# Dilated attention in a decoder trunk: Q and K of six head pairs made in a seven-product phase ahead of the heads, stored split, and loaded a head ahead

## The chip, the cores and the metric

One Trainium2 chip, one core of it (core 0). The metric is the device time of one execution in microseconds; before the change its median is 2148.01 us over three runs (2147.04 to 2149.72). Profiled executions are taken by the hardware profiler.

## The reference

Two layers on a sequence of 1024 tokens with width 1024, all in float32: layer 0 mixes tokens with a gated short convolution, layer 1 with dilated attention (16 heads of 64), and each is followed by a SwiGLU network of width 2816. What the change touches is the projection to q, k, v and the three branches of attention:

```python
BRANCHES = ((128, 1), (512, 4), (2048, 16))   # window, dilation

def dilated_attention_mixer(h, w_qkv, w_out, rel_bias):
    bsz, seq, _ = h.shape
    qkv = (h @ w_qkv).reshape(bsz, seq, 3, N_HEADS, HEAD_DIM)
    q, k, v = qkv[:, :, 0], qkv[:, :, 1], qkv[:, :, 2]
    outs, lses = [], []
    for window, dilation in BRANCHES:
        o, l = dilated_branch(q, k, v, rel_bias, window, dilation)
        outs.append(o)
        lses.append(l)
    alpha = jax.nn.softmax(jnp.stack(lses, axis=0), axis=0)
    o = jnp.sum(alpha[..., None] * jnp.stack(outs, axis=0), axis=0)
    return o.reshape(bsz, seq, D_MODEL).astype(h.dtype) @ w_out
```

Here `h` is the RMS-normalised residual. In a branch, query t attends to the keys t - j * dilation, with a bias per head and distance.

## The kernel before

Activations lie transposed: a tile X[n] holds 128 features by 1024 tokens. A float32 value is written as a sum of two parts (hi and lo, `split`, L139 on ScalarE and L140 on DVE), and a product is three matmuls: hi x hi, hi x lo, lo x hi. Weights come in slabs of 128 x 1024 (`add_slab`, `take`), are split a few steps ahead and then used.

Two forms of product are in use. The plain one (`product`, L364 to L366) runs 8 blocks of 128 features and two halves of 512 tokens. The other (class `Strassen`, L553 to L555) takes a pair of slabs as a 2 x 2 block matrix and makes seven products in place of eight: each product is 4 blocks x 3 matmuls of 128x512, with sums of weight blocks (`combo`, L187) and of activation blocks made on DVE ahead, and sums of results behind. The short convolution (class `Conv`, with its own order of products) and the SwiGLU networks use it; Q, K, V and the output projection of attention use the plain form.

Four engines work in queues that each run in the order of the program: TensorE (PE), VectorE (DVE), ScalarE (ACT) and GpSimd (POOL); SyncE (SP) issues most loads. The order is written by hand: the program interleaves Python generators, and what it issues first on an engine runs first there.

Attention runs over 16 heads in slots. `qkv(p)` makes Q and K of pair p (part 1 is K) in the plain form, in 36 units: a unit is one step of `product` (three matmuls of 128x512) or the end of a product; `evacuate` multiplies by the norm's 1/rms out of PSUM (L1359, L1361). It also makes value tiles (`value_tiles`, L1395 to L1397, 20 units for each half g, j). Pair 0 and the first value tiles come ahead of the slots. `split_kq(p)` splits K and Q of both heads of a pair on ScalarE and DVE (L1424, L1425) and copies the keys regrouped by their distance mod 4 into KC (`kca`, `kcb`).

In slot n, TensorE runs the scores of head n (`scores`, eight steps, the first of which read KC), interleaved with the values of head n-1 (`values`, L1529) and every second step with one unit of filler (`dense`); then the remaining fillers. The softmax of head n goes meanwhile over DVE (biases added, maxima L1506, L1507), POOL (an all-reduce of the maximum over partitions, L1510), DVE (five subtractions, L1518) and ScalarE (five exponentials, L1519). In the second loop of a slot the order within one step i is:

```python
            for i in range(8):
                if a == 1 and i == 2:
                    attended()
                if a == 1 or i < FIN0 or i > SOFT:
                    next(extra, None)
                if i == SOFT:
                    if a == 1:
                        run(extra)
                    if n < H:
                        live[n] = new
                        run(softmax(new))
```

with SOFT = 4; in odd slots `extra` is split_kq of the next pair. The fillers are Q, K and values of the next pairs (27 units per slot, 29 in slot 12), then the output projection of five pairs (`out_product`, 24 units in slot 14, 22 in 15, 20 behind).

Ahead of the slots, the last loop of the first SwiGLU network adds up X[n] and calls `Norm.add`, which makes h_hi and h_lo of whole tiles (L423, L424) and the squares for the norm; `Norm.stats` makes 1/rms on TensorE, ScalarE and DVE. X[n] is then stored (`spill`).

Of the kernel before, what the change touches and what calls it, by code (L numbers as in the profile page):

```python
# [17 lines left out]
S = 1024  # L18
# [24 lines left out]
CONV = "conv"  # L43
# [4 lines left out]
AO = 5  # L48
DEEP_ORDER = (1, 2, 5, 6, 7, 3, 4)
# [46 lines left out]
def trunk(ctx: ExitStack, tc: tile.TileContext, x, gains_in, cwi, ck, cwo, wqkv, wo, relb,  # L96
# [181 lines left out]
    def add_units(key, nu, column):  # L278

        units, slabs, base = [], {}, len(raw_src)  # L280
        raw_base[key] = base
        for u in range(nu):
            if key == CONV:
# [6 lines left out]
            if key == CONV:  # L290
# [19 lines left out]
            if key != CONV and u > 4 and u % 2:  # L310
# [3 lines left out]
        ops.extend(units[u][m] for u, m in unit_order(nu, key == CONV))  # L314
# [26 lines left out]
    for p in range(NPAIR):  # L341
        for part in (1, 0):
            add_slab(("qkv", p, part), wqkv[part * KT + p])
        if p == 0 or p % 2 and p < NPAIR - 1:
            for j in range(2):
                add_slab(("v", (p + 1) // 2, j), wqkv[2 * KT + (p + 1) // 2 * 2 + j])
# [174 lines left out]
    class Strassen:  # L521
# [4 lines left out]
        def __init__(self, key, norm, nu, pairs, chunk, tiles, source):  # L526
            self.key, self.norm, self.nu, self.order = key, norm, nu, unit_order(nu, key == CONV)
# [53 lines left out]
        def products(self, filled, hooks={}):  # L581

            for n, (u, m) in enumerate(self.order):
# [3 lines left out]
                elif self.key != CONV and u > 3:  # L587
# [7 lines left out]
        def whole(self, u, m, d):  # L595
# [16 lines left out]
            if m == 2 and u > 4 or (u, m) == (0, 4) or self.key == CONV and (u, m) == (3, 7):  # L612
# [238 lines left out]
    class Conv(Strassen):  # L851
# [28 lines left out]
        def operands(self):  # L880
            gain, stt = self.norm.gain, nc.vector.scalar_tensor_tensor
            a, b = half(0), half(1)
# [5 lines left out]
            yield  # L888
            t3, t2 = [half_page("t3") for k in range(4)], [half_page("t2") for k in range(4)]
# [140 lines left out]
        def mix(self, group1):  # L1030
# [62 lines left out]
            group1("co", self.plain, self.hid)  # L1093

# [241 lines left out]
    def attention(norm):  # L1336
# [8 lines left out]
        by_time = lambda t: view(t, 0, [[1, 16], [16, 32]])  # L1345
        by_residue = lambda t: view(t, 0, [[32, 16], [1, 32]])

        parts = {}

        def qkv(p, first=False):  # L1350

            parts[p] = {}
            held = []

            def evacuate(part, h, b):
                rstd = norm.rstd[:, half(h)]
                t = parts[p][part, h] = half_page("kq")
                if part == 1:
                    nc.vector.tensor_tensor(out=by_time(t), in0=by_residue(b), in1=by_residue(rstd), op=ALU.mult)  # L1359
                else:  # L1360
# [576 lines left out]
```

## Time and profile before

| | |
|---|---|
| median of three runs | 2148.01 us |
| span of the profiled execution | 2146.3 us |
| mean clock of TensorE, as granted | 0.996 |
| first projection matmul of attention | 970.5 us |
| first scores of head 0 | 1020.6 us |
| first scores of head 15 | 1417.9 us |
| Q and K, three rows L364, L365, L366 | 768 matmuls of 128x512 |

A row of a timeline has its start in us from the span's start, its duration, the engine, the line of the kernel, the operation, what it writes and reads, its shape, and in brackets how long the engine stood idle before it and whom it waited for. `x3` are three instructions merged. A row of a stretch has its length and, for each engine, busy time and instructions. In a row of a group stand the times in total, the mean in ns, and idle time before. A row of a tile has the least, median and longest duration in ns, and the first and the last start. PEld is the loading of weights into TensorE.

### The profile page before, as it was taken

To read this page: it belongs to the slowest core of one execution; us is meant where nothing else is said; L and a number is where in the kernel's file an instruction comes from. 1 tells how busy PE (TensorE), PEld (TensorE's weight loads), DVE (VectorE), ACT (ScalarE), POOL (GpSimd) and SP (SyncE) were. 2 spreads that over 40 slices of the span, in tenths; PEclk is the share of its full clock that TensorE was granted. 3 is DMA by queue.
4 is the path that set the end of the run, shared out by engine and by line. 5 is a ranking of instruction groups with operands and counts; after the bars stand their busy time and mean duration, and the time that the engine had idled before them with its cause. 6 is when DMAs were issued, how large, how long until landed. Compare 5 with 4: busy or idle time off the path is not lost. (4 is left out here: it accounts for less than half of the span.)

```text
span 2146.3 us, 30609 instructions
## 1 busy us (share of the span) xinstructions
PE 2121.9 (99%) x11158; PEld 1820.2 (85%) x11158; DVE 1721.2 (80%) x3192; ACT 1012.7 (47%) x1836; POOL 183.6 (9%) x239
## 2 busy tenths in 40 slices
PE   9999999999999999999999999999999999999998
PEld 7788888888888888878999999887788888888887
DVE  8898769988888888864777777877998888888886
ACT  7333426443434464334555555535543444456435
POOL 1000000111101000010111111111010101001000
PEclk9999999999999999999999999999999999999999
DMA  7322642233233576323333333646223332368432
GB/s 217 94 93 69 226 137 69 107 110 104 103 109 113 173 228 189 100 65 128 83 93 94 93 95 84 193 128 180 64 83 105 113 108 104 102 205 232 163 94 79
DMA packets 135055, 264.49 MB, mean 123 GB/s; under 512 B 47912, under 2 KB 59192, under 8 KB 134906
## 3 DMA queue, kind: packets, MB, share of 16 engines
q1 hardware_dynamic: 74106, 177.99, 26.1%
q0 software_dynamic: 19632, 61.46, 9.2%
q10 hardware_dynamic: 41168, 23.10, 3.6%
q8 instruction: 88, 1.44, 0.3%
q14 instruction: 61, 0.50, 0.1%
HBM read 188.88 MB, written 66.27 MB: 119 GB/s over the span
## 5 line engine op out<-in xcount | busy, mean ns | idle before, releaser
L555 PE MATMUL bank<-b,w 128*128 128x512 f32 x1784 | 696.4, 390 | 3.6 <-DVE w L140 3.6
L553 PE MATMUL bank<-b,w 128*128 128x512 f32 x1784 | 698.4, 391 | 1.2 <-ACT w L139 1.0
L554 PE MATMUL bank<-b,w 128*128 128x512 f32 x1784 | 696.6, 390 | 2.9 <-DVE b L546 2.2
L555 PEld LDWEIGHTS bank<-b,w 128*128 128x128 f32 x1784 | 335.8, 188 | 75.7 <-DVE w L140 5.7
L554 PEld LDWEIGHTS bank<-b,w 128*128 128x128 f32 x1784 | 336.1, 188 | 73.2 <-DVE b L546 2.9
L553 PEld LDWEIGHTS bank<-b,w 128*128 128x128 f32 x1784 | 336.2, 188 | 71.0 <-ACT w L139 1.4
L139 ACT ACTIVATE w<-combo 128x512 fp32r<-128x512 f32 (+2 forms) x464 | 234.6, 537 | 218.0 <-DVE combo L187 201.3
L140 DVE TENSOR_TENSOR w<-combo,w 128x512 fp32r<-128x512 f32 (+2 forms) x464 | 261.1, 577 | 36.9 <-ACT w L139 36.3
L559 ACT ACTIVATE part<-bank 128x512 f32<-128x512 f32 x168 | 100.3, 598 | 375.9 <-PE bank L555 374.2
L140 DVE TENSOR_TENSOR w<-raw,w 128x512 fp32r<-128x512 f32 (+2 forms) x316 | 171.0, 563 | 35.8 <-ACT w L139 35.8
L563 DVE TENSOR_TENSOR part<-part,bank 128x256 f32<-128x256 f32 (+1 forms) x348 | 159.2, 490 | 28.7 <-PE bank L555 16.6
L139 ACT ACTIVATE w<-raw 128x512 fp32r<-128x512 f32 (+2 forms) x316 | 151.0, 521 | 45.5 <-PE bank L555 11.5
L364 PE MATMUL bank<-w_hi,w 128*128 128x512 f32 (+1 forms) x320 | 119.7, 374 | 1.0 <-ACT w L139 1.0
L366 PE MATMUL bank<-w_hi,w 128*128 128x512 f32 (+1 forms) x320 | 118.0, 369 | 0.7 <-DVE w L140 0.7
L365 PE MATMUL bank<-w_lo,w 128*128 128x512 f32 (+1 forms) x320 | 117.8, 368 | 0.0
L783 DVE TENSOR_TENSOR x<-x,bank 128x512 f32<-128x512 f32 x136 | 93.2, 685 | 29.6 <-PE bank L555 29.6
L486 DVE TENSOR_TENSOR x<-x,bank 128x512 f32<-128x512 f32 (+1 forms) x104 | 66.1, 643 | 51.8 <-PE bank L366 51.2
L364 PE MATMUL bank<-h_hi,w_hi 128*128 128x512 f32 x256 | 104.6, 409 | 0.1
L187 DVE TENSOR_TENSOR combo<-raw 128x512 f32<-128x512 f32 (+1 forms) x160 | 103.4, 646 | 0.0
L366 PE MATMUL bank<-h_hi,w_lo 128*128 128x512 f32 x256 | 100.2, 391 | 0.7 <-DVE w_lo L140 0.7
L365 PE MATMUL bank<-h_lo,w_hi 128*128 128x512 f32 x256 | 100.1, 391 | 0.0
L1552 ACT ACTIVATE z<-bank 64x512 f32<-64x512 f32 x32 | 19.0, 595 | 145.2 <-PE bank L1529 145.2
(261 smaller groups left out, 3892.6 us busy)
## 6 DMA issues: line engine op xcount, KB each, us to landing
hin<-part SPq DMA_DIRECT2D x126, 256.0 KB
raw<-in_ffn_w_gate SPq DMA_DIRECT2D x44, 512.0 KB
raw<-in_ffn_w_up SPq DMA_DIRECT2D x44, 512.0 KB
part<-sum POOLq DMA_DIRECT2D x72, 256.0 KB, 2.3
raw<-in_ffn_w_down SPq DMA_DIRECT2D x48, 384.0 KB
raw<-in_conv_w_in SPq DMA_DIRECT2D x24, 512.0 KB
raw<-in_attn_w_qkv SPq DMA_DIRECT2D x24, 512.0 KB
part<-part POOLq DMA_DIRECT2D x36, 256.0 KB, 2.4
```

Of the source, the lines that this page charges most:

```text
L139: nc.scalar.activation(hi, src, AF.Copy)
L140: eng.tensor_tensor(out=lo, in0=src, in1=hi, op=ALU.subtract)
L187: eng.tensor_tensor(out=c, in0=a, in1=b, op=op)
L364: nc.tensor.matmul(b, whi[:, a], ahi[:, s], start=first, stop=False)
L365: nc.tensor.matmul(b, whi[:, a], alo[:, s], start=False, stop=False)
L366: nc.tensor.matmul(b, wlo[:, a], ahi[:, s], start=False, stop=last)
L553: nc.tensor.matmul(b, hi[:, a], bhi, start=start and k == 0, stop=False, skip_group_check=True)
L554: nc.tensor.matmul(b, hi[:, a], blo, start=False, stop=False, skip_group_check=True)
L555: nc.tensor.matmul(b, lo[:, a], bhi, start=False, stop=k == n - 1, skip_group_check=True)
L559: nc.scalar.activation(t, b, AF.Copy)
L563: nc.vector.tensor_tensor(out=t, in0=t, in1=b, op=ALU.add)
L783: nc.vector.tensor_tensor(out=X[n][:, half(h)], in0=X[n][:, half(h)], in1=b, op=ALU.add)
```

## The change

K and Q of pairs 0 to 5 are no longer made by `qkv` among the heads, but in a phase of their own (class `QueryKey`, `mix`) between the first SwiGLU network and the heads. A unit u is pair u with its slabs of K and Q as the 2 x 2 block matrix; the phase has 42 products in the order of the short convolution. Results are scaled, split and written to memory (`emit`). The blocks of activations are made from X by `operand` in the loop before (`tail`) and by `differences`; four of them (b[1], b[2], b[3], and b[8] made late) serve as h for the values and for pairs 6 and 7. Those two pairs stay in the plain form as fillers (`projections`), stored by `emit` too.

In slot n, `load_kq(n + 1)` loads the next head's keys and queries, split as they are, on SP's queue; `classes(n + 1)` copies the regrouped keys on ScalarE. The fillers are now v1, v2, qk6, v3, qk7 and the output projection; 15 units in each of slots 0 to 12, 20 behind. The values' first group comes ahead of slot 0.

```diff
-CONV = "conv"
+CONV, QK = "conv", "qk"
+QK_PAIRS = 6
...
+FILL = (("v", 0), ("v", 1), ("v", 2), ("qk", 6), ("v", 3), ("qk", 7))
...
+    class QueryKey(Conv):
+        def __init__(self, norm):
+            Strassen.__init__(self, QK, norm, QK_PAIRS, 0, 1, 0, None)
+            self.waiting, self.ready = [], False
+            self.kq = {(p, part): dram.tile([256, S], F32, name=f"kq{p}_{part}")
+                       for p in range(NPAIR) for part in range(2)}
+        def tail(self, n):
+            self.operand(1 + n // 4, n % 4, n, X[n][:, half(0)])
+            self.norm.square(n)
+            nc.scalar.dma_start(spill[n], X[n])
+        def emit(self, p, part, h, v):
+            t, rstd = half_page("kq"), self.norm.rstd[:, half(h)]
+            if part == 1:
+                nc.vector.tensor_tensor(out=by_time(t), in0=by_residue(v), in1=by_residue(rstd), op=ALU.mult)
+            else:
+                nc.vector.scalar_tensor_tensor(t, v, 0.125, rstd, op0=ALU.mult, op1=ALU.mult)
+            yield 1
+            to = self.kq[p, part]
+            hi, lo = half_page("kq_hi", F32R), half_page("kq_lo", F32R)
+            split(t, (hi, lo))
+            nc.gpsimd.dma_start(to[:128, half(h)], hi.bitcast(F32))
+            nc.gpsimd.dma_start(to[128:, half(h)], lo.bitcast(F32))
+            yield 1
...
+            self.products(filled, {(1, 2): gather, (3, 1): spread, (5, 1): load, (5, 7): last_operand})
+            self.h = [[self.b[1 + 7 * h * (k < 4) + (1 + h) * (k > 3)][k % 4] for k in range(KT)] for h in range(2)]
+            self.step(None)
...
-        def split_kq(p):
...
+        def load_kq(n):
+            p, a = divmod(n, 2)
+            k, q = qk.kq[p, 1], qk.kq[p, 0]
+            rows = lambda t, r: bass.AP(t.tensor, t.offset + r * S, [[S, 64], [1, S]])
+            n0, n1 = (slice(64 * i, 64 * i + 64) for i in (a, 1 - a))
+            KS[n], QS[n] = page("ka", F32R), page("qa", F32R)
+            nc.sync.dma_start(KS[n][n0].bitcast(F32), rows(k, 64 * a))
+            nc.sync.dma_start(KS[n][n1].bitcast(F32), rows(k, 128 + 64 * a))
+            for m in (n0, n1):
+                nc.sync.dma_start(QS[n][m].bitcast(F32), rows(q, 64 * a))
+            nc.sync.dma_start(qlo[a][n0].bitcast(F32), rows(q, 128 + 64 * a))
+        def classes(n):
+            KC[n] = page("kca", F32R)
+            for h in range(2):
+                nc.scalar.activation(KC[n][:, half(h)], view(KS[n], h * HALF, [[1, 4], [4, 128]]), AF.Copy)
+                yield
...
+                load_kq(n + 1)
...
-            if a == 1 and p + 1 < NPAIR:
-                extra = split_kq(p + 1)
+            if n + 1 < H:
+                later = classes(n + 1)
...
-                if a == 1 or i < FIN0 or i > SOFT:
+                if i < FIN0 or i > SOFT:
                     next(extra, None)
+                if i > SOFT:
+                    next(later, None)
                 if i == SOFT:
-                    if a == 1:
-                        run(extra)
                     if n < H:
                         live[n] = new
                         run(softmax(new))
...
+        load_kq(0)
+        for j in range(2):
+            run(value_tiles(0, j))
+        run(classes(0))
...
+        dense = fill()
+        for n in range(H):
+            if n == H - 4:
+                done.update(load_attended(range(AO)))
+            hook = halves() if n == H - 4 else iter(())
+            slot(n, dense, 20 if n > H - 4 else 15, 3 if n == H - 2 else 0, hook)
             run(hook)
...
         def after(n):
-            norm.add(n)
+            qk.tail(n)
...
         sw.feed_forward(*rest, after)
+        qk.mix()
```

More of the change, by code (lines that the diff above doesn't have):

```diff
@@ L313, in add_units @@
         raw_src.extend(slabs[r] for r in range(len(slabs)))
-        ops.extend(units[u][m] for u, m in unit_order(nu, key == CONV))
+        ops.extend(units[u][m] for u, m in unit_order(nu, early))
     def add_down(key, w, pairs, chunk, last):
@@ L586, in products @@
                     self.deeper(u, m - DEEPER)
-                elif self.key != CONV and u > 3:
+                elif not self.early and u > 3:
                     self.shallow(u, m, d)
@@ L880, in operands @@
         def operands(self):
[L881 to L882 removed]
+            a = half(0)
             for k in range(4):
@@ L888, in operands, with differences @@
             yield
+            yield from self.differences()
+        def differences(self):
+            gain, stt = self.norm.gain, nc.vector.scalar_tensor_tensor
+            a, b = half(0), half(1)
             t3, t2 = [half_page("t3") for k in range(4)], [half_page("t2") for k in range(4)]
@@ L1343, in attention, with projections @@
         nc.vector.memset(vx[:, :, 64:128], 1.0)
[L1345 to L1360, printed above, removed]
-                    nc.vector.scalar_tensor_tensor(t, b, 0.125, rstd, op0=ALU.mult, op1=ALU.mult)
-            stats = None
+        def projections(p):
+            late = []
             for part in (1, 0):
```

184 lines of the change are left out of this document (106 added, 78 removed).

## The prediction

> **What bounds the kernel now.** I read the page's first lines, then one window over the attention blocks, then timelines of single engines.
>
> ```profile
> span 2146.3 us, 30609 instructions
> ...
> PE 2121.9 (99%) x11158; PEld 1820.2 (85%) x11158; DVE 1721.2 (80%) x3192; ACT 1012.7 (47%) x1836; POOL 183.6 (9%) x239
> ```
>
> ```profile
> 1010.00:1410.00 400.00, 397.50 (x2672) 364.51 (x2672) 289.43 (x473) 206.83 (x303) 51.67 (x21) 1.00 0.37 104
> ```
>
> The second row gives the stretch, its length, the busy time of PE, PEld, DVE, ACT and POOL, the clock, the DMA share and GB/s. TensorE hardly ever waits, in the blocks of the heads either (2.5 us idle in 400), so now every matmul costs and the other engines work under its cover. A matmul's price is the step from start to start, since matmuls overlap. The timeline of TensorE:
>
> ```profile
> 1089.81 0.39 PE L364 MATMUL bank<-h_hi,w_hi 128*128 128x512 f32 x1
> ...
> 1094.34 0.39 PE L366 MATMUL bank<-h_hi,w_lo 128*128 128x512 f32 x1
> ...
> 1109.83 0.28 PE L1395 MATMUL bank<-w_hi,h_hi 128*128 128x256 f32 x1
> ...
> 1121.23 0.28 PE L1397 MATMUL bank<-w_hi,h_lo 128*128 128x256 f32 x1
> ...
> 1122.04 0.28 PE L1456 MATMUL bank<-qa,kca 128*128 128x256 f32 x1
> ...
> 1133.17 0.28 PE L1457 MATMUL bank<-ql,ka 128*128 128x128 f32 x1
> ...
> 1134.14 0.47 PE L364 MATMUL bank<-h_hi,w_hi 128*128 128x512 f32 x1
> ...
> 1147.83 0.28 PE L1456 MATMUL bank<-qb,kcb 128*128 128x256 f32 x1
> ```
>
> The first two rows span 20 steps of 128x512: 0.2265 us each (the records say 0.39). The next two span the 95 steps of a value tile's 96 matmuls: 0.12 us each. The last four are one slot: head n's first scores at 1122.04, its last scores at 1133.17, the last values at 1134.14, the next head's first scores at 1147.83. Everything between 1134.14 and 1147.83 is filler, and it is this filler that hides the softmax.
>
> **What the softmax needs, in that slot.** DVE, then POOL, then DVE and ScalarE again:
>
> ```profile
> 1133.48 0.42 DVE L1493 TENSOR_TENSOR ld<-bank,bias 128x256 f32<-128x256 f32 x1 [0.55 <-PE bank L1457]
> ...
> 1134.74 0.69 DVE L1507 TENSOR_TENSOR m<-m,lp 128x512 f32<-128x512 f32 x1
> ...
> 1138.85 1.23 DVE L1518 TENSOR_TENSOR lf<-lf,mb 128x1024 f32<-128x1024 f32 x1 [0.65 <-POOL mb L1510]
> ```
>
> ```profile
> 1135.60 3.22 POOL L1510 PARTITION_ALL_REDUCE mb<-m  x1 [20.53 <-issue]
> ```
>
> ```profile
> 1140.11 1.06 ACT L1519 ACTIVATE lf<-lf 128x1024 f32<-128x1024 f32 x1 [4.47 <-DMA vx<-vdram]
> ...
> 1142.81 1.03 ACT L1519 ACTIVATE lp<-lp 128x384 f32<-128x384 f32 x2
> 1143.75 1.99 ACT L139 ACTIVATE w_hi<-raw 128x1024 fp32r<-128x1024 f32 x2
> ```
>
> From the head's first scores to the first subtraction 16.8 us; from there to the moment when ScalarE is free of the five exponentials 4.9 us more (1143.75): 21.7 us after the first scores. Today nothing of the next head's scores hangs on that, because the regrouped keys of both its heads were copied ahead of the exponentials, in this order on ScalarE:
>
> ```profile
> 1172.39 1.16 ACT L1425 ACTIVATE kca<-ka 128x512 fp32r<-128x512 f32 x1
> ...
> 1174.51 1.05 ACT L1519 ACTIVATE lf<-lf 128x1024 f32<-128x1024 f32 x1
> ```
>
> **What the change removes.** 6 pairs x 96 matmuls of 128x512 become 42 products x 12 = 504, so 72 fewer: 72 x 0.2265 = 16.3 us. The work of split_kq and of h_hi and h_lo over whole pages goes too; that was under TensorE's cover and gives nothing by itself. The extra stores (two POOL issues per half, 48 in all) and loads (five SP issues and 1.3 MB per head) I cost at nothing: they are asked for a slot, some 20 us, ahead, with the engines 0.37 busy in the window above. Without that cover each us that the keys are late is a us per slot. The eight spills of x go from ahead of the blocks into the FFN's last loop, on ScalarE's queue, which is less than half busy over the span; I take nothing for them either.
>
> **What it moves.** The fillers of a slot fall from 27 units to 15, and the copy of the regrouped keys (now `classes`) is called in the slot's loop only at i > SOFT, behind `softmax` at i == SOFT. ScalarE takes its queue in order, so the first scores of head n+1 wait for: five exponentials, then the copy. On TensorE these scores stand ahead of the values of head n, of the fillers and of everything after, so all wait with them; DVE's first additions of the head wait for these scores. Behind the copy on ScalarE stand only a value tile's copies and those of z and o, and for these nobody waits so early.
>
> A slot's TensorE work: 12.1 us from 1122.04 to 1134.14 less its three fillers (2.0) is 10.1; fifteen units of values are 12 x 6 x 0.12 = 8.6, of Q and K 13.3 x 3 x 0.2265 = 9.1: 18.9 us. A slot's chain: 21.7 + 1.16 for the copy + 0.1 = 23.0. Some queues have a value copy (0.48) or weight splits (1.99) between the last exponential and the copy, mean 0.4; the value fillers in the first part are lighter by about as much. So **TensorE idles 4.1 us in each such slot**, and the slot lasts 23.0 us. Bounds for that +-0.5.
>
> **What an idle gap does to the clock.** Two places of the trace show it:
>
> ```profile
> 1501.75 0.40 PE L553 MATMUL bank<-b,w 128*128 128x512 f32 x1
> 1504.37 0.61 PE L554 MATMUL bank<-b,w 128*128 128x512 f32 x1 [2.22 <-DVE b L546]
> 1504.78 0.63 PE L555 MATMUL bank<-b,w 128*128 128x512 f32 x1
> ```
>
> ```profile
> 1504.40:1511.20 6.80, 6.80 (x21) 5.62 (x22) 5.80 (x10) 2.40 (x6) 0.84 (x1) 0.52 0.29 52
> ```
>
> ```profile
> 23.00:30.00 7.00, 5.34 (x16) 3.70 (x15) 6.83 (x12) 6.04 (x10) 0.00 (x0) 0.76 0.02 6
> ```
>
> A gap of 2.22 us was followed by 6.8 us at clock 0.52: 3.3 us lost. Around 25 us, 1.66 us of idle time in 7 brought the mean clock to 0.76: 1.7 us lost. A 4.1 us gap is longer than either. The slow time then lies in the next slot's first part, which is on the chain (11 us from first to last scores). I take the middle of the two, 2.4 us per gap; bounds 0 and 3.3.
>
> The Trainium skill, "TensorE: Matmul & The Clock Gate", section "What's actually happening", has the clock halve after one idle window of about 3.4 us, free-running, and its last table holds gaps below some 3 us harmless. That speaks for few drops: a whole window fits into a 4.1 us gap in one case of five. The trace disagrees, since 2.22 us was enough there.
>
> **DVE in the new phase.** Counted from the instruction order, the 42 products carry 115.5 us of DVE work (steps below: 0.60 for a 128x512 pass, 0.69 with a gain, 0.95 for a reordered key) against 114.2 us of matmuls (504 x 0.2265).
>
> ```profile
> 1520.37 3.70 DVE L546 TENSOR_TENSOR b<-x,b 128x512 fp32r<-128x512 f32 x6
> ```
>
> ```profile
> 53.48 2.74 DVE L864 SCALAR_TENSOR_TENSOR b<-x,gains,b 128x512 fp32r<-128x512 f32 x4
> ```
>
> ```profile
> 997.62 1.98 DVE L1359 TENSOR_TENSOR kq<-bank,rstd 128x512 f32<-128x512 f32 x2 [5.33 <-ACT rstd L482]
> ```
>
> ```profile
> 20.00:40.00 20.00, 18.34 (x73) 14.41 (x72) 18.39 (x30) 16.43 (x26) 3.44 (x4) 0.91 0.57 144
> 40.00:60.00 20.00, 18.94 (x84) 15.37 (x83) 18.70 (x31) 12.57 (x22) 1.69 (x2) 1.00 0.65 154
> ...
> 100.00:120.00 20.00, 20.00 (x90) 16.57 (x89) 19.86 (x41) 7.01 (x12) 1.11 (x2) 1.00 0.24 80
> ```
>
> The short convolution runs the same order of products. There DVE at 19.86 of 20 us costs TensorE nothing, since weights are split two products ahead; only the stage that makes the operands (20 to 60) lost 2.7 us. I take 3 us, bounds 0 and 8.
>
> **The sum.** One stretch holds all that changes: from the first projection matmul to the first scores of head 15.
>
> ```profile
> 970.51 0.39 PE L364 MATMUL bank<-h_hi,w_hi 128*128 128x512 f32 x1
> ```
>
> ```profile
> 1417.93 0.28 PE L1456 MATMUL bank<-qb,kcb 128*128 128x256 f32 x1
> ```
>
> That is 447.4 us before. After: 114.2 for the products; 3.7 for the norm's sums (rows below, 1.84 + 1.88); 3 for DVE; 23.0 for value tiles 0 (192 x 0.12); 1.9 of idle time while the last value copy and then the first regrouping run (0.2 + 0.48 + 1.16); slot 0, without values, 21.2 (13.5 from 1020.61 to the subtraction at 1034.1, 1.1 for a weight split more on DVE, then 4.9 + 0.48 + 1.16 + 0.1); slots 1 to 12 12 x 23.0 = 276; slots 13 and 14, with 20 units of 0.68 us, are as long as their TensorE work, 10.1 + 13.6, 47.4; the clock 13 x 2.4 = 31.2. Sum 521.6, so 74.2 us more. Behind that point 37 units are left where 36 were.
>
> ```profile
> 988.58 1.84 PE L465 MATMUL bank<-ones,acc 128*128 128x1 f32 x16
> 995.87 1.88 PE L481 MATMUL bank<-diag,ones 128*128 128x512 f32 x4
> ...
> 1020.61 0.29 PE L1456 MATMUL bank<-qa,kca 128*128 128x256 f32 x1
> ```
>
> ```profile
> 1020.81 0.48 ACT L1400 ACTIVATE v<-bank,r 128x256 f32<-128x256 f32 x1 [2.40 <-PE bank L1397]
> ```
>
> ```profile
> L140 DVE TENSOR_TENSOR w_lo<-raw,w_hi 128x1024 fp32r<-128x1024 f32 x24 | 28.7, 1224 | 27.1 <-ACT w_hi L139 27.1
> ```
>
> ```profile
> L1510 POOL PARTITION_ALL_REDUCE mb<-m x16: 3217/3224/3227, 1030.8 to 1431.2; - x16
> L1518 DVE TENSOR_TENSOR lf<-lf,mb x16: 1220/1226/1227, 1034.1 to 1436.0; 128x1024 f32<-128x1024 f32 x16
> ```
>
> The span would be 2146.3 + 74.2 = 2220.5. The median of the runs, 2148.0, lies 1.7 above the span: **2222 us**.
>
> **The rivals.**
>
> 1. The clock stays up: gaps of 4.1 us, no drop, 2222 - 31 = 2191 us. For it: the trace has only two drops, and the 1.06 us of idle time in 40 to 60 left the clock at 1.00. Against it: the 2.22 us gap. By the skill's window rule one gap in five drops it, 2191 + 13 x 2.4 / 5 = 2197 us, so this case has that price too.
>
> 2. The new phase is held by DVE as well. In 20 to 60 DVE reached 37.1 of 40 us with TensorE waiting; at that rate 115.5 us take 124.5, and a clock drop or two come on top: 14 us in place of 3, 2233 us. Against it: 100 to 120.
>
> 3. The other side, faster: the chain of the slot stays within 18.9 us, so that TensorE is never without work. The place is ScalarE's copy of the regrouped keys; it decides from 4.1 us on that the copy must be earlier. Then the slots cost their matmuls, the stretch gives back 16.3 us and about 3 us of today's idle time against 3 + 1.9 for the new phase: 2134 us. For it: subtractions can begin as soon as POOL is done, and some slots are lighter. Against it: the sum of measured passes in order, with no pass left out, is 23.0.
>
> That the matmuls are not fewer can be excluded: the loops issue 504 for 576.
>
> **How the numbers follow.** The forecast 0.60, clock up 0.20, DVE too 0.12, the other side 0.06, no difference by chance 0.02. Without the clock, DVE and 0.5 us in each of 15 slots the time is 2222 - 31 - 3 - 7.5 = 2181; with 3.3 per gap (+12), 8 for DVE (+5) and 0.5 per slot (+7.5) it is 2247. The range of 2181 to 2247 holds the first three cases. Within 0.2% (4.3 us) a measurement of this kernel tells nothing; faster 0.06, same 0.02, slower 0.92.
>
> **What would show it.** Regrouping copies directly behind the last exponential, and TensorE's first scores of each head waiting for them by about 4 us; the interval of the all-reduces near 25 us in the first 13 slots (26.7 before: 1030.8 to 1431.2 is 15 intervals); granted clock well below 1 in those slots and 1.00 in the new phase; 72 fewer 128x512 matmuls; TensorE busy in slots 13 and 14. I am wrong if first scores start without a wait on ScalarE, if another wait (a load of keys) ends later than the copy, or if the phase takes over 125 us.

## The result, and the profile after

The changed kernel takes 2253.36 us (median of four, 2250.24 to 2255.20) against 2147.53 of the kernel before (2145.21 to 2149.72): a ratio of 1.049 (95% interval 1.048 to 1.051). It is slower, as forecast, but by 31 us more than forecast, and 6 us above the top of the stated range (2247). The profile page's first lines, with the clock that TensorE was granted in 40 slices, and one window over the slots, with the columns of the windows above:

```profile
span 2250.5 us, 30931 instructions
...
PE 2143.5 (95%) x11086; PEld 1834.9 (82%) x11086; DVE 1752.9 (78%) x3272; ACT 1004.3 (45%) x1848; POOL 219.1 (10%) x303
...
PEclk9999999999999999999998899899999999999999
```

```profile
1130.00:1530.00 400.00, 325.10 (x2198) 305.01 (x2197) 231.90 (x408) 151.91 (x217) 61.71 (x37) 0.89 0.59 153
```

72 matmuls are gone (11158 less 11086), but in 400 us of slots TensorE now stands idle for 74.9 where it was 2.5, and the clock is 0.89. TensorE's waits from the new phase to the last slot (us in total, times, longest):

```profile
PE bank L1544 <- ACT kca L1528: 60.7, 13, 9.4
PE bank L1489 <- ACT w_hi L141: 7.6, 2, 6.3
PE bank L369 <- ACT w_hi L141: 5.7, 1, 5.7
PE bank L562 <- DVE w L142: 5.4, 6, 1.5
PE bank L560 <- ACT part L566: 5.3, 2, 3.0
```

The first row is the wait that was forecast. One of the 13 is head 0's (1.56 us, forecast as part of the transition); the other twelve last 4.9 us on average, where 4.1 was forecast. One of them in the timelines, ScalarE's rows, then TensorE's:

```profile
1254.11 1.06 ACT L1607 ACTIVATE lf<-lf 128x1024 f32<-128x1024 f32 x1 [1.28 <-DVE lf L1606]
...
1257.74 2.10 ACT L1528 ACTIVATE kca<-ka 128x512 fp32r<-128x512 f32 x2
```

```profile
1258.88 0.58 PE L1544 MATMUL bank<-qa,kca 128*128 128x256 f32 x1 [4.78 <-ACT kca L1528]
```

The exponentials, directly behind them the copies, and the next head's scores as soon as the first copy is done. Where the stretch of the forecast's sum goes is read from four rows of TensorE's timeline, the first product, the first value tile, and the first scores of heads 0 and 15:

```profile
968.75 0.39 PE L560 MATMUL bank<-b,w 128*128 128x512 f32 x1
...
1104.30 0.28 PE L1489 MATMUL bank<-w_hi,b 128*128 128x256 f32 x1
...
1133.26 0.39 PE L1544 MATMUL bank<-qa,kca 128*128 128x256 f32 x1 [1.56 <-ACT kca L1528]
...
1523.62 0.28 PE L1544 MATMUL bank<-qa,kca 128*128 128x256 f32 x1
```

| part of the stretch | forecast | measured | more |
|---|---|---|---|
| new phase (114.2 + 3.7 + 3) | 120.9 | 135.6 | 14.7 |
| value tiles 0 and the first regrouping (23.0 + 1.9) | 24.9 | 29.0 | 4.1 |
| slot 0 | 21.2 | 22.7 | 1.5 |
| slots 1 to 12, clock among it (276 + 12 x 2.4) | 304.8 | 317.0 | 12.2 |
| slots 13 and 14 (47.4 + 2.4) | 49.8 | 50.7 | 0.9 |
| sum | 521.6 | 554.9 | 33.3 |

The stretch begins 1.8 us earlier than in the kernel before and what follows it is 1.5 shorter, so the span is 30.0 over the forecast. Two rows of the table carry it.

**The phase.** VectorE's waits from 968 to 1104 us, and one product in the timelines of VectorE and ScalarE:

```profile
DVE kq_lo L142 <- ACT kq_hi L141: 15.3, 21, 0.8
```

```profile
1053.06 1.05 DVE L1128 TENSOR_TENSOR kq<-part,rstd 128x512 f32<-128x512 f32 x1
1054.86 0.69 DVE L142 TENSOR_TENSOR kq_lo<-kq,kq_hi 128x512 fp32r<-128x512 f32 x1 [0.75 <-ACT kq_hi L141]
```

```profile
1054.19 0.63 ACT L141 ACTIVATE kq_hi<-kq 128x512 fp32r<-128x512 f32 x1 [1.98 <-issue]
1054.73 0.61 ACT L141 ACTIVATE w<-combo 128x512 fp32r<-128x512 f32 x1
```

VectorE scales a half, ScalarE rounds it, VectorE subtracts: VectorE stands 0.75 us in between, and the next weights' rounding stands behind kq_hi on ScalarE. My 115.5 us counted VectorE's passes (in the trace VectorE is busy for 114.0 of the phase's 135.6 us) and not these stops. TensorE is idle for 11.3 us of the phase; the fourth and fifth of its waits above, for split weights and for saved results, are nearly all of that.

**The slots.** First scores to first scores, read from TensorE's timeline: slots 1, 3, 4, 5 and 7 to 10 last 24.1 to 26.2 us, 25.1 on average (forecast 23.0 + 2.4). Slots 2, 6, 11 and 12 last 28.1, 29.6, 27.8 and 30.5, 14.4 us over four times 25.4. Rows of ScalarE and TensorE in slot 2; of GpSimd, ScalarE (ACTq: it issues a load) and VectorE in slot 6; of ScalarE in slot 11; of TensorE in slot 12:

```profile
1204.54 1.99 ACT L141 ACTIVATE w_hi<-raw 128x1024 fp32r<-128x1024 f32 x2
```

```profile
1205.63 0.58 PE L1489 MATMUL bank<-w_hi,b 128*128 128x256 f32 x1 [6.28 <-ACT w_hi L141]
```

```profile
1300.49 3.22 POOL L1598 PARTITION_ALL_REDUCE mb<-m  x1 [13.11 <-DVE m L1595]
```

```profile
1301.60 0.63 ACTq L1506 DMA_DIRECT2D vx<-vdram  x1
1302.27 1.56 ACTq L1508 DMA_DIRECT2D vx<-vdram  x2
1303.87 2.01 ACT L141 ACTIVATE w_hi<-raw 128x1024 fp32r<-128x1024 f32 x2 [3.28 <-DMA vx<-vdram]
```

```profile
1304.96 2.36 DVE L142 TENSOR_TENSOR w_lo<-raw,w_hi 128x1024 fp32r<-128x1024 f32 x2 [2.49 <-ACT w_hi L141]
...
1307.84 1.22 DVE L1606 TENSOR_TENSOR lf<-lf,mb 128x1024 f32<-128x1024 f32 x1
```

```profile
1439.57 1.35 ACT L141 ACTIVATE w_hi<-raw 128x640 fp32r<-128x640 f32 x2
1440.82 0.61 ACT L141 ACTIVATE kq_hi<-kq 128x512 fp32r<-128x512 f32 x1
1441.34 2.12 ACT L1528 ACTIVATE kca<-ka 128x512 fp32r<-128x512 f32 x2
```

```profile
1466.72 0.80 PE L369 MATMUL bank<-w_hi 128*128 128x512 f32 x1 [5.69 <-ACT w_hi L141]
```

In slots 2 and 12 the rounding of a filler's operands stands behind the exponentials, so TensorE waits at the filler (6.28 and 5.69 us), and the next scores, which stand behind it, start late without a wait of their own. In slot 11 the roundings of a filler's weights and of a key half (1.35 and 0.61 us) stand between the last exponential and the copy. In slot 6 the subtractions begin 4.1 us after the all-reduce has ended (1303.71), behind weight splits that waited for ScalarE, which was issuing the loads of the values.

### The profile page after: what moved, and what is told of

It reads as the page before. It is cut to its first block, busy times and chain, and to the rows that moved or that the text cites. A ratio compares the mean times of both kernels' runs of the same rounds, so it can differ in the third digit from the quotient of the medians.

```text
span 2250.5 us, 30931 instructions
## 1 busy us (share of the span) xinstructions
PE 2143.5 (95%) x11086; PEld 1834.9 (82%) x11086; DVE 1752.9 (78%) x3272; ACT 1004.3 (45%) x1848; POOL 219.1 (10%) x303
## 5 line engine op out<-in xcount | busy, mean ns | idle before, releaser
L560 PE MATMUL bank<-b,w 128*128 128x512 f32 x1952 | 766.0, 392 | 7.0 <-ACT part L566 5.3
L562 PE MATMUL bank<-b,w 128*128 128x512 f32 x1952 | 763.1, 391 | 8.9 <-DVE w L142 8.8
L561 PE MATMUL bank<-b,w 128*128 128x512 f32 x1952 | 763.0, 391 | 2.5 <-DVE b L553 2.2
L562 PEld LDWEIGHTS bank<-b,w 128*128 128x128 f32 x1952 | 367.8, 188 | 91.9 <-DVE w L142 15.3
L560 PEld LDWEIGHTS bank<-b,w 128*128 128x128 f32 x1952 | 367.8, 188 | 86.5 <-ACT part L566 6.9
L561 PEld LDWEIGHTS bank<-b,w 128*128 128x128 f32 x1952 | 368.1, 189 | 79.1 <-DVE b L553 3.1
L141 ACT ACTIVATE w<-combo 128x512 fp32r<-128x512 f32 (+2 forms) x488 | 248.9, 540 | 222.1 <-DVE combo L189 205.3
L142 DVE TENSOR_TENSOR w<-combo,w 128x512 fp32r<-128x512 f32 (+2 forms) x488 | 276.1, 579 | 38.0 <-ACT w L141 37.3
L142 DVE TENSOR_TENSOR w<-raw,w 128x512 fp32r<-128x512 f32 (+2 forms) x334 | 182.1, 566 | 37.5 <-ACT w L141 37.5
L570 DVE TENSOR_TENSOR part<-part,bank 128x256 f32<-128x256 f32 (+1 forms) x366 | 170.4, 495 | 30.1 <-PE bank L562 16.7
L1544 PE MATMUL bank<-qa,kca 128*128 128x256 f32 (+1 forms) x128 | 40.9, 343 | 60.7 <-ACT kca L1528 60.7
L553 DVE TENSOR_TENSOR b<-hin,b 128x512 fp32r<-128x512 f32 x126 | 79.5, 683 | 9.3 <-ACT b L552 9.0
L1489 PE MATMUL bank<-w_hi,b 128*128 128x256 f32 x256 | 78.4, 306 | 7.6 <-ACT w_hi L141 7.6
L1555 DVE TENSOR_TENSOR lf<-bank,bias 128x256 f32<-128x256 f32 x64 | 24.0, 418 | 77.2 <-PE bank L1545 63.8
```

The costliest lines, as they stand in the source:

```text
L141: nc.scalar.activation(hi, src, AF.Copy)
L142: eng.tensor_tensor(out=lo, in0=src, in1=hi, op=ALU.subtract)
L560: nc.tensor.matmul(b, hi[:, a], bhi, start=start and k == 0, stop=False, skip_group_check=True)
L561: nc.tensor.matmul(b, hi[:, a], blo, start=False, stop=False, skip_group_check=True)
L562: nc.tensor.matmul(b, lo[:, a], bhi, start=False, stop=k == n - 1, skip_group_check=True)
L570: nc.vector.tensor_tensor(out=t, in0=t, in1=b, op=ALU.add)
```

## The experiments

Each kernel was timed in four runs beside seven of the kernel before (medians 2145.0 to 2146.7 in the four groups of runs). The diffs are against the changed kernel unless another is named.

### 1. The copy ahead of the exponentials

```diff
-                if i > SOFT:
+                if i in (SOFT - 2, SOFT - 1):
                     next(later, None)
```

> The regrouping copies of head n+1 go ahead of the five exponentials of head n on ScalarE (steps 2 and 3 of the slot's second part in place of those behind the softmax); nothing else changes. Theory (the slot's chain ends in the copy): TensorE's waits for the copy, 60.7 us in 13 places, fall below 10 us; the slots of 25.4 to 26.3 us shrink to the larger of their TensorE work (18.9) and of first scores to first exponential (16.8 + 1.2 + 1.1 = 19.1), about 20; 13 slots x 5.8 = 75 us less, about 2178 us (2160 to 2195), the clock near 1.00 in the slots. Rival (the keys' loads or the thinner fillers set the slot, whatever the order on ScalarE): slots stay above 24 us and the time above 2230.

Measured: 2228.21 us, 1.038 (1.037 to 1.040): 25 us less, a third of what was expected, and outside the range of either theory. TensorE's waits for the copy, then ScalarE's for the keys:

```profile
PE bank L1544 <- ACT kca L1528: 10.9, 4, 4.8
```

```profile
ACT kca L1528 <- DMA ka<-kq: 54.6, 6, 11.3
```

The copy is the end of the chain, and right behind it stands a second wait, hidden by the first: in six odd slots the keys land 5.9 to 11.3 us after ScalarE has come to the copy, and the exponentials then wait with it.

### 2. The copy later

```diff
-            for h in range(2):
+            for h in (0, 0, 0, 1) if 0 < n < 14 else (0, 1):
                 nc.scalar.activation(KC[n][:, half(h)], view(KS[n], h * HALF, [[1, 4], [4, 128]]), AF.Copy)
-                yield
+                if h or n == 0:
+                    yield
```

> The opposite of the first: in slots 0 to 12 the first regrouping copy of the next head is made three times over (into the same place), so it ends 2.1 us later behind the exponentials. Theory (the copy ends the chain of the slot): 13 x 2.1 = 27 us more, about 2280 us (2275 to 2286). Rival (something else ends last and the copy has slack): under 10 us more, below 2263.

Measured: 2275.30 us, 1.061 (1.059 to 1.062): 22 us more. From head 0's first scores to head 13's it is 365.4 us (1131.8 to 1497.2) for 339.7 (1133.3 to 1473.0): 25.7 for 13 delays, 2.0 each. Of that, slot 13 gives some back (24.5 for 27.2). The delay of the copy goes nearly one to one into the slot.

### 3. The low half one product later

```diff
             to = self.kq[p, part]
             hi, lo = half_page("kq_hi", F32R), half_page("kq_lo", F32R)
-            split(t, (hi, lo))
+            nc.scalar.activation(hi, t, AF.Copy)
+            yield 0
+            nc.vector.tensor_tensor(out=lo, in0=t, in1=hi, op=ALU.subtract)
```

(The `yield 1` ahead of these lines goes. The lines also serve the two pairs made in the slots.)

> In the new phase alone: the low half of a query or key half is subtracted one product later than its high half is rounded, so that VectorE does not stand still while ScalarE rounds. Theory (24 waits of VectorE for kq_hi, 0.70 to 0.76 us each, some 17 us in all, put VectorE over the matmuls' time): the phase shrinks from 135.6 us (first product 968.75 to first value tile 1104.30) to about 121, the time falls by 14 us, to about 2239 (2233 to 2244). Rival (the waits of TensorE in the phase come from the saves and weight splits on ScalarE, or from VectorE's passes alone): less than 5 us, above 2248.

Measured: 2249.38 us, 1.048 (1.047 to 1.050), 4 us less; a miss, and the phase is no shorter (136.4 us for 135.6). VectorE's waits in the phase, and a product in the timelines of ScalarE and VectorE:

```profile
DVE w L142 <- ACT w L141: 18.3, 19, 1.3
```

```profile
1052.91 0.63 ACT L1133 ACTIVATE kq_hi<-kq 128x512 fp32r<-128x512 f32 x1 [1.89 <-issue]
1053.45 0.62 ACT L141 ACTIVATE w<-combo 128x512 fp32r<-128x512 f32 x1
```

```profile
1054.10 0.69 DVE L142 TENSOR_TENSOR w<-combo,w 128x512 fp32r<-128x512 f32 x1 [1.27 <-ACT w L141]
```

The wait for kq_hi went, and one for the weights came: they are rounded behind kq_hi on ScalarE, and kq_hi still waits for the scaling on VectorE. The ring (scaling, rounding, subtraction and, behind the rounding, the next weights) was longer than the edit.

### 4. Both halves one product later

```diff
+        def spaced(self, p, part, h, v):
+            t, rstd = half_page("kq"), self.norm.rstd[:, half(h)]
+            self.round()
...
+            self.rest()
+            self.held.append([t, self.kq[p, part], h])
+            yield 2
```

(`round` makes the high half of what is held, `rest` its low half and the two stores; the scaling stands between them, where the dots are.)

> In the new phase alone (the two pairs made in the slots as before the edit): both the rounding of a query or key half on ScalarE and the subtraction of its low half on VectorE are issued one product later than its scaling, the rounding ahead of the next scaling and the subtraction behind it. e2 had moved the wait (VectorE 1.27 us per product for the rounded weights, which stood behind the high half on ScalarE). Theory (the phase is held by the passing to and fro between VectorE and ScalarE once per product, not by the sum of either's passes): the phase falls from 135.6 us to about 121 (118 to 126), the time to about 2239 us (2234 to 2244). Rival (saves that keep banks, or VectorE's own sum, hold it): phase above 131, time above 2248.

Measured: 2230.49 us, 1.040 (1.038 to 1.042): 23 us less, more than expected. The first product, the first value tile and head 0's first scores in TensorE's timeline:

```profile
968.12 0.39 PE L560 MATMUL bank<-b,w 128*128 128x512 f32 x1
...
1089.29 0.28 PE L1515 MATMUL bank<-w_hi,b 128*128 128x256 f32 x1
...
1114.41 0.39 PE L1570 MATMUL bank<-qa,kca 128*128 128x256 f32 x1 [1.56 <-ACT kca L1554]
```

The phase takes 121.2 us (forecast 120.9) and the transition 25.1 (24.9). VectorE makes the same passes, and is still busy for 111.8 us of the phase, without holding TensorE, whose idle time there falls from 11.3 us to 2.1. So the passing to and fro cost 14.4 us in the phase and 3.8 in the transition, where the value weights were split late behind it. (Of the 3.8, 1.5 is chance: the same short gap brought the clock down in the changed kernel and did not in experiments 2, 10 and 12, where the transition takes 27.5.)

### 5. First and third edit together

> Both edits. Theory (two separate stretches, so the gains add): 2253 - 75 - 14 = 2164 us (2146 to 2180). Rival (the phase's gain is given back at the first slot, where the keys come later than the matmuls): the gain of the two is under 80 us, above 2173.

Measured: 2236.54 us, 1.041 (1.040 to 1.043), 8 us slower than the first edit alone. The rival's sign is right, but not its reason: from head 0's to head 15's first scores the two kernels take the same, 368.9 us here and 369.1 in experiment 1. Nothing is given back in the slots, and the third edit had nothing to add, since the phase is as long as in experiment 3 (136.4 us). The two profiled executions lie 4.9 us apart: 1.4 of it in phase and transition, 1.8 ahead of the phase and 1.9 behind head 15's first scores, where neither edit changes anything. What makes the rest of the 8 us stays open.

### 6. Keys and queries asked for two heads ahead

```diff
# against experiment 1
             run(sc)
             run(pv)
+            if n + 2 < H and n + 2 != 14:
+                load_kq(n + 2)
```

(At the slot's start only head 14 is left to be loaded; heads 0 and 1 are loaded ahead of the slots.)

> e1 with the loads of the keys and queries of head n+2 issued in the middle of slot n (behind its scores) in place of those of head n+1 at its start; head 14, whose keys are made in slot 12, is still asked for one slot ahead. Theory (what was left in e1 were the keys' loads, 54.6 us of ScalarE's waits in six odd slots): ScalarE's waits for them fall below 15 us, TensorE's for qa, kca, lf and ld behind them from 44 to below 15, the time from 2228 to about 2190 us (2175 to 2205). Rival (loads and exponentials only share a place: the chain of VectorE, GpSimd and ScalarE still needs over 22 us per slot): above 2215.

Measured: 2214.42 us, 1.032 (1.031 to 1.034): 14 us under experiment 1, at the edge of the rival's 2215. ScalarE waits 8.7 us for keys in place of 54.6. VectorE's waits, and one in its timeline:

```profile
DVE o L1704 <- DMA z<-rdram: 32.3, 5, 11.3
```

```profile
1259.51 1.23 DVE L1704 TENSOR_TENSOR o<-o,z 128x1024 f32<-128x1024 f32 x1 [5.42 <-DMA z<-rdram]
1260.65 1.22 DVE L1606 TENSOR_TENSOR lf<-lf,mb 128x1024 f32<-128x1024 f32 x1
```

A third wait: the subtractions stand behind the product o x z (`attended`), to which VectorE now comes before z has landed, in five odd slots. It is there in experiment 1 too (28.0 us in five places), where the changed kernel has 4.8.

### 7. The gap filled with matmuls

```diff
+            if n < 13:
+                hi, lo = qk.h[0][0]
+                b = bank()
+                for _ in range(16):
+                    nc.tensor.matmul(b, hi[:, :128], lo, start=True, stop=True)
             run(extra)
```

> The changed kernel with 16 idle products more per slot (slots 0 to 12, behind the fillers, into a bank that nobody reads): 3.6 us of matmuls in the gap ahead of the next head's first scores, and nothing else changed. Theory (the gap halves the clock and the slow matmuls of the next slot's first part lie on the chain): the half-clock stretches in the slots go for the most part, first scores to first exponential shrinks from some 20.5 to 18 us, 12 x 2.4 = 29 us less, about 2224 us (2212 to 2236). Rival 1 (the clock's drop lies in slack): 2253, no change. Rival 2 (the products push the next scores out): slower, up to 2270.

Measured: 2241.94 us, 1.045 (1.043 to 1.046): 11 us less with 208 matmuls more; above the theory's range. Windows from head 5's first scores on, as long as this kernel needs to its all-reduce, in the changed kernel and in this one, and below them the changed kernel in 2 us windows around one gap:

```profile
1258.88:1272.18 13.30, 13.30 (x98) 13.30 (x99) 6.36 (x15) 2.50 (x4) 0.00 (x0) 0.84 0.62 140
```

```profile
1261.60:1274.90 13.30, 13.30 (x113) 13.21 (x114) 8.23 (x18) 3.61 (x7) 0.00 (x0) 1.00 0.62 141
```

```profile
1230.00:1232.00 2.00, 0.00 (x0) 0.00 (x0) 1.18 (x3) 1.86 (x3) 0.00 (x0) 1.00 0.98 312
1232.00:1234.00 2.00, 0.46 (x2) 0.46 (x3) 0.00 (x0) 2.00 (x4) 0.00 (x0) 0.63 1.06 265
1234.00:1236.00 2.00, 2.00 (x11) 2.00 (x11) 0.76 (x2) 0.86 (x2) 0.00 (x0) 0.50 0.90 215
...
1238.00:1240.00 2.00, 2.00 (x14) 2.00 (x14) 0.75 (x2) 0.00 (x0) 0.00 (x0) 0.66 0.57 144
1240.00:1242.00 2.00, 2.00 (x19) 2.00 (x19) 1.18 (x2) 0.00 (x0) 0.00 (x0) 1.00 0.00 0
```

At full clock 113 matmuls fit where 98 did, and head 5's all-reduce starts 13.4 us after its first scores (15.4 before). The slots of heads 4, 5, 8 and 9 then last 22.7 to 23.4 us: that is the forecast's 23.0 without a clock term. At the end of three of them TensorE still waits 0.7 to 1.1 us for the copy, so it is the chain that sets them and not the added products. The gain is smaller than 12 such steps for two reasons: in five places TensorE still waits 3.65 to 6.65 us and the clock falls, and the products lengthen slots in which TensorE was not waiting for the copy alone: 28.1 to 30.3 in slot 2, 30.5 to 32.3 in slot 12.

### 8. Experiments 4 and 6 together

> e5 and e6 together. Theory (separate stretches): 2253 less the gains of e5 and e6, about 2176 us (2160 to 2192). Rival (they interfere, as e1 and e2 did): above 2200.

Measured: 2195.65 us, 1.023 (1.022 to 1.025). From experiment 6 it is 18.8 less, from the changed kernel 57.7 where the two gave 22.9 and 38.9: they add to within 4.1 us. It lies above its range all the same, because the 2176 had been reckoned with larger gains of the two.

### 9. Weights split at the start of a slot

```diff
+            if n < 13:
+                ensure(min(op_state[1] + 2, first_ao - 1))
             if n < H:
```

> The changed kernel with the splits of the next weights (up to two operations beyond the one in use) issued at the start of a slot, ahead of its scores, in place of wherever a filler reaches them; the copies of the keys stay behind the exponentials. Theory (in four slots, heads 2, 6, 11 and 12, weight splits stand between all-reduce and copy on ScalarE and VectorE, and these slots last 28.1, 29.6, 27.8 and 30.5 us where the rest last 25.4): the four fall to about 25.4 each, 14 us less, about 2239 us (2233 to 2245). Rival (splits take their time wherever they stand, or the weights arrive too late for an earlier split): above 2249.

Measured: 2251.86 us, 1.0485 (1.0468 to 1.0503): no change. Slots 2, 6 and 11 come down (27.1, 25.3 and 26.5), slot 12 stays (30.1), and slots 3 and 4 grow to 28.3 each: their all-reduces start 17.9 and 19.0 us after the first scores (14.5 to 16.1 for heads 1 to 12 of the changed kernel), and in slot 4 VectorE stands still for 3.94 us between two of the head's additions while TensorE works on. Why it does was not settled. So the place of the splits matters, but this edit moved the cost; what a harmless split would give stays open.

### 10. Loads of the values from SyncE's queue

```diff
-                nc.scalar.dma_start(vx[...], ...)
+                nc.sync.dma_start(vx[...], ...)
```

> The changed kernel with the loads of the values issued from SyncE's queue in place of ScalarE's; nothing else changed. Theory (in slot 6 the six loads kept ScalarE from two weight splits for 3.3 us, VectorE waited 2.5 us for these and its subtractions began 4.1 us after the all-reduce): slot 6 falls from 29.6 to about 26, the other slots stay, the time falls by 3 to 4 us, about 2249 us. Rival (the loads on SyncE come behind its own waits and the values start late): slower, 2258 or more.

Measured: 2245.59 us, 1.047 (1.045 to 1.049): 8 us less, twice the theory. Slot 6 falls from 29.6 to 26.9; slots 9 to 11 fall by 1.3 to 2.2 each, slots 7 and 8 grow by 1.5 and 0.5. Not all of it is the edit's: the transition's 1.5 us less is the chance of the clock (experiment 4), and slot 9 lasts 23.3 to 23.8 in experiments 3, 4 and 12 as well, where 25.6 stands in the changed kernel and 23.5 here.

### 11. Experiments 8 and 9 together, and then five pairs

> e8 with the splits of e9. Theory (TensorE's waits in e8 for weights rounded behind the exponentials, 6.4 and 6.5 us, go, and with them their half-clock stretches): 2195.7 - 13 = about 2183 us (2174 to 2190). Rival (the softmax's chain sets these slots too): above 2190.

Measured: 2204.64 us, 1.0274 (1.0254 to 1.0295), 9 us slower than experiment 8; the rival. TensorE's waits for copies are back (18.8 us in six places).

```diff
# against it
-QK_PAIRS = 6
+QK_PAIRS = 5
...
-            slot(n, dense, 20 if n > H - 4 else 15, 3 if n == H - 2 else 0, hook)
+            slot(n, dense, 20 if n > H - 4 else 13 if n == H - 4 else 18, 3 if n == H - 2 else 0, hook)
```

(Three pairs are now made in the slots; their first heads, 10, 12 and 14, are loaded one head ahead.)

> e11 with five pairs in the new phase in place of six, and 18 fillers per slot in place of 15. Theory (the change takes cover out of slots whose softmax chain does not get shorter): the phase is 84 products' matmuls shorter, 19.0 us, the slots of 23.8 us on average in e8 hold three fillers more (2.0 us) without growing, so the time falls by 13 to 19 us against e11, to about 2167 us (2158 to 2176). Rival (TensorE's work sets the slots of e11): slots grow by 2 us, the time by 13 x 2.0 - 19.0 = 7 us against e11.

Measured: 2208.96 us, 1.030 (1.028 to 1.031), 4 us more, near the rival's 7: the phase is 17.2 us shorter, and from head 0's to head 15's first scores it is 16.3 longer. This does not show that TensorE's work sets the slots: ScalarE waits 34.0 us in three places for keys again, and these are as many as the heads loaded one slot later, so the two causes are mixed.

### 12. Slot 12 without the attended pages

```diff
-            slot(n, dense, 20 if n > H - 4 else 15, 3 if n == H - 2 else 0, hook)
+            slot(n, dense, 20 if n > H - 4 else 12 if n == H - 4 else 15, 3 if n == H - 2 else 0, hook)
             run(hook)
+            if n == H - 4:
+                next(dense)
```

> The changed kernel with 12 fillers in slot 12 in place of 15, and one more behind the splits of the attended pages: the last fillers of slot 12 are products with these pages (the fillers ahead of them end after 12.8 slots), and their halves are rounded behind the exponentials. Theory (slot 12's 30.5 us are TensorE's 5.7 us wait for these halves and the slow clock after it): slot 12 falls to 25 to 26 us, three fillers of 0.7 us move to slot 13, so 3 to 5 us less, about 2249 us (2245 to 2252). Rival (the next slot waits in its place): 2253, no change.

Measured: 2254.05 us, 1.051 (1.049 to 1.053): no change. Slot 12 falls from 30.5 to 26.4 as expected, but slots 13 and 14 grow from 27.2 and 23.5 to 29.0 and 26.0.

### 13. The order repaired further

Three kernels, each on the one before: experiment 8 with experiment 12 and `attended()` behind the softmax; with the loads of experiment 10; with one weight split at the start of slot 2.

```diff
# against experiment 8
-                if a == 1 and i == 2:
-                    attended()
...
             run(extra)
+            if a == 1:
+                attended()
```

> e8 with e13's edit and with the product o x z of the attended pages behind the softmax of the odd slots in place of ahead of it. Theory (in e8 VectorE waits 32.0 us in five odd slots for z's load, and the subtractions stand behind that wait): the waits of values for exponentials, 30.0 us in e8, fall below 12, slots 5, 7, 9 and 11 (21.5 to 26.3 us there) come down to about 20, the time from 2195.7 to about 2170 us (2160 to 2182). Rival (a wait of the same length takes its place, because the chain of VectorE itself is over 22 us): above 2186.

> e14 with the loads of the values on SyncE's queue (as e10, which gave 8 us). Theory (ScalarE's 15 us of waits ahead of the copies go): 4 to 8 us under e14. Rival (SyncE's queue, which carries keys and z as well, is the bound): e14 or slower.

> e15 with the weights of the third value tile pair split at the start of slot 2. Theory (TensorE's 6.4 us wait in slot 2 goes, with the half clock after it): 5 to 8 us under e15, about 2158 us if e14 and e15 hold; above the kernel before in any case, since slots of 20 us with 18.9 us of work leave some 13 us that 16.3 us of saved matmuls do not pay with the clock's losses. Rival (order alone makes up the whole loss): at or below 2145.

Measured: 2189.13 us, 1.021 (1.019 to 1.022); 2179.90 us, 1.016 (1.015 to 1.018); 2181.19 us, 1.017 (1.015 to 1.018). The first misses its range by 7 us: TensorE's waits for exponentials fall to 13.7 us, but in slots 12 and 13 it waits 20.3 for operands of the output projection. The second gains 9.2 us, a little more than its 4 to 8. The third is a miss: slot 2 falls from 26.4 to 18.5, and slots 3, 4, 7 and 9 take it back. The same eight slots, heads 3 to 10, in the changed kernel and in the second of the three:

```profile
1209.40:1414.73 205.33, 167.09 (x1169) 159.94 (x1168) 115.67 (x206) 76.07 (x113) 33.04 (x20) 0.89 0.55 139
```

```profile
1182.70:1338.60 155.90, 151.55 (x1169) 145.99 (x1169) 110.48 (x201) 74.47 (x109) 32.33 (x20) 0.98 0.66 172
```

The same 1169 matmuls take 25.7 us per slot there and 19.5 here (155.90 / 8), near the 18.9 of the forecast's TensorE work. So in these slots order alone made the loss. The other slots still last 26.5 and 26.4 (1, 2), 24.2, 26.6, 34.3 and 26.9 (11 to 14); against 19.5 and, for 13 and 14, 23.7 that is 39.5 us, somewhat more than the 35 that this kernel lies above the one before. The longest wait there is for head 14's keys, which are made in slot 12, in ScalarE's timeline:

```profile
1420.35 1.11 ACT L1554 ACTIVATE kca<-ka 128x512 fp32r<-128x512 f32 x1 [15.36 <-DMA ka<-kq]
```

No version beat the kernel before. Whether these six slots could be repaired too was not tried.

## Why the prediction was right, and where it was wrong

The direction and the wait were right, the time was not: 2253.36 us lies above the range of 2181 to 2247. Of the prediction's own signs of being wrong one came true, since the phase takes more than 125 us; and the all-reduces of heads 0 to 13 lie 26.6 us apart, where 25 was forecast.

- **Direction and mechanism: right.** The copy behind the exponentials ends the slot's chain (60.7 us in 13 waits); experiment 1 took most of them away (10.9 us in four were left, though other waits came in their place), experiment 2 lengthened them nearly one to one.
- **The slot's 23.0 us: right.** Where the clock stayed up (experiment 7) undisturbed slots last 22.7 to 23.4. The 19.5 of experiment 13 is close to TensorE's 18.9.
- **The clock, 2.4 us per gap: nearly right.** From first scores to all-reduce it takes 15.3 us on average for heads 1 to 12, and 13.3 to 13.4 for seven of these heads in experiment 7, where the clock stayed up: 1.9 to 2.0 per gap. (The middle of 1.7 and 3.3 is 2.5 and not 2.4, 1 us in the sum.) The first rival (clock up) is out: each of the 13 gaps of 3.46 us and more in the slots brought it down, where the rival had one in five.
- **"DVE in the new phase ... I take 3 us, bounds 0 and 8": wrong, and the largest miss.** Measured 17.7 (135.6 less 114.2 and 3.7), and 4.1 more in the transition. The step that failed is the comparison with the short convolution by the sum of passes. Its results are not split as they come out; here each result goes from VectorE to ScalarE and back within one product, and the weights' rounding queues behind it. With the subtraction and the rounding moved one product back (experiment 4) the same passes cost 3.3 us, within the bounds, and the kernel takes 2230.49 us, inside the range. The second rival had the size (14) from the wrong cause: VectorE's sum of passes did not hold the phase.
- **"mean 0.4", "Bounds for that +-0.5": mis-sized.** The mean slot hid four in which weight splits, or the values' loads, stand between all-reduce and copy or hold the fillers back: 14.4 us together. Experiment 10 took 2.6 of slot 6's; slots 2 and 12 could be shortened (experiments 13 and 12), though others took it back, so the net worth of these splits stays open.
- **Loads "at nothing": right for this order only.** With the copy behind the exponentials ScalarE never waited for keys, which had landed by then; with the copy ahead of them they cost 54.6 us of ScalarE's time (experiment 1).
- **Not in the sum:** in slot 0 ScalarE issues loads of the values until 1149.2, and a value copy and an ACT_TABLE_LOAD of 1.28 us come behind them, ahead of the exponentials. These start 2.8 us after the first subtraction, and 1.25 after it in experiment 10, which moves the loads away; that explains most of slot 0's 1.5.

## What to carry to other kernels

Before work is moved out of a pipelined loop, walk the longest chain of what stays with every instruction that stands ahead of it on each in-order queue, slot by slot and not by the mean: the cover that was taken away had hidden several waits one behind the other, and repairing one shows the next. A busy sum tells how long an engine needs when nothing is passed back to it within a step; where one engine's result returns through another, count the stops, or issue the return one step later. Test an order with a pair of kernels, the suspect earlier and later: the gain of the first is bounded by the next wait, the loss of the second is the slope.

## What the runs showed of the hardware

- The clock fell within a gap of 3.66 us (idle from 1229.88 to 1233.54, the windows of experiment 7): 1232 to 1234 has 0.63 and the next window 0.50, so it fell about 2.6 us after the last matmul, and it came back between 1238 and 1240. All 13 gaps of 3.46 to 9.40 us in the slots are followed by such a stretch, and so is one of 2.99 us in the phase (at 1061.78), but not one of 2.69 (at 1500.13). Around 3 us and below, the length alone does not decide: 2.22 us brought the clock down in the kernel before (at 1504.37) and 1.40 us in experiment 2 (at 1041.60), while 3.02 us in experiment 7 (at 1063.15) did not.

  The stretches with the gaps of 2.99 and 2.69:

```profile
1060.00:1070.00 10.00, 8.22 (x29) 6.66 (x30) 7.73 (x13) 3.94 (x7) 2.72 (x6) 0.83 0.65 227
1500.00:1510.00 10.00, 9.87 (x83) 9.73 (x84) 6.99 (x16) 2.91 (x5) 0.00 (x0) 1.00 0.82 199
```

  The Trainium skill ("TensorE: Matmul & The Clock Gate", section "What's actually happening") has it fall after an idle window of 3.4 us at a free-running phase. In this trace it fell in or just behind all 13 gaps, from 2.3 us after the last matmul (the gap that ends at 1258.88) to 5.1 (the one that ends at 1388.54), so in some of them earlier than after 3.4.
- Six loads issued from ScalarE's queue, from 1299.45 to 1303.8 us, kept a rounding there waiting 3.28 us (slot 6); issuing takes that engine's time in its order even though the profile does not count it as busy.
